# The order of the pointwise stage: two z splits and a silu earlier, the low halves of the output weight behind them

## The chip, the cores and the metric

The kernel runs on one core of a Trainium2 chip, as one program. The metric is the device time of one execution in microseconds (us); less is better. Before the change the median of three runs is 470.81 us (470.47 to 470.90).

## The reference

The reference is one layer of a hybrid streaming encoder in float32, for 1024 prompt tokens and 64 tokens of a running stream. One input projection yields queries, keys, values, two SiLU gates and a GLU pair. Group A is sliding-window attention; group B is a convolution module. Each group's output is RMS-normalised, multiplied by its gate, and both go through the shared output projection. Cut to the part around the change:

```python
def _conv_branch(u, left, conv_w, ln_g, ln_b, w_pw):
    h = _dwconv(jnp.concatenate([left, u], axis=1), conv_w)
    h = jax.nn.silu(_layernorm(h, ln_g, ln_b))
    return h @ w_pw                                   # the pointwise stage

def _merge(att, ga, conv, gb, g_att, g_conv, w_out, g_post):
    y = jnp.concatenate([_rms(att, g_att) * jax.nn.silu(ga),
                         _rms(conv, g_conv) * jax.nn.silu(gb)], axis=-1) @ w_out
    return _rms(y, g_post)
```

## The kernel before

Matrix products keep float32 accuracy by splitting each operand into a high part, rounded to the format that TensorE reads at full rate, and a low part, which is the rest (original minus high). A product is then three products: high by high, low by high and high by low. The high part of something is one copy; the low part is one subtraction with two inputs in SBUF.

The kernel has four stretches: the input projection (with the convolution's taps on VectorE beside it), attention, the pointwise stage, and the output projection, tokens in tiles of 128 (`y` in the profile, T = 0, 1, 8, 2, ..., 7).

The pointwise stage (lines 1097 to 1114) works on H, which holds the normalised convolution output, channels on the partitions, tokens along the row. Its tokens are cut into four ranges n = 0 to 3 of 280, 280, 280 and 278 columns (`LNC`), and for each range there are four output channel blocks m = 0 to 3: 16 products `pointwise(n, m)` (lines 572 to 590), written pw(n,m) below, each of 12 matmuls, which are four for high weight by zh, four for low weight by zh, four for high weight by zl. Where a range is ready, three things have been done to it:

- `S` (`silu`, line 557): four ScalarE activations on H, in place.
- `z` (`split_z`, line 562): VectorE makes zh (a copy) and zl (a subtraction). The tiles for zh and zl have two buffers each, so z2 needs the buffers of z0, which are free when pw(0,3) has been computed, and z3 those of z1, free behind pw(1,3).

Behind each product VectorE multiplies its result by the gate and puts it into H (`H<-pw,gb`), ScalarE squares the result (`csq<-pw`, for m = 0 `sqc<-pw`), and for m = 1 to 3 GpSimd adds that square to a running sum (`sqc<-sqc,csq`). The results rotate through seven PSUM banks.

Into this stage is also put the preparation of the output weight w_out, in eight pieces i = 0 to 7 (lines 1025 to 1051): `h` (`wo_hi`) is its high part on ScalarE, `l` (`wo_lo`) its low part on VectorE. Pieces 0, 3 and 6 are handled in two halves. At its end `wo_lo(i)` issues the load of piece i+3 on SyncE's DMA queue. Further tasks are `G` (gate of the attention output), `M` and `n` (high and low part, `mh` and `ml`, of the merged activations of an output tile; `M0` on ScalarE, `n0` on VectorE) and `r` (the reciprocal root of the group norm).

The order is written out by hand: the list `plan` (line 1110) has 16 entries, and entry 4n+m names the tasks that are issued directly behind pw(n,m). All instructions of this stage are pinned, that is, each engine gets its own in exactly the order in which the program issues them, and each engine works its queue in order. Before the loop z0, z1, S0, S1, the gates, piece 0 and the high part of piece 1 are already issued.

The first output product, T = 0, begins with one matmul on `mh` of the convolution half and goes on with one on `ml` of that half, which n0 writes second.

Of the kernel before, what the change touches and what calls it, by code (L numbers as in the profile page):

```python
# [48 lines left out]
def layer_kernel(ctx: ExitStack, tc: tile.TileContext, x, x_fm, w_in, w_pw, w_out, vec, g_post,  # L49
# [704 lines left out]
    h1, h2 = (0, 4), (4, KT)  # L754
# [352 lines left out]
    drain()  # L1107
    run_due(lambda p: True)

    plan = "G0,l1,h2 l2,h3 l3,S2 h4 z2 l4,h5 l5,S3 h6 z3,h7 l6,M0 l7 n0 r0 . M1 n1".split()  # L1110
    for n in range(4):
        for m in range(4):
            pointwise(n, m, [pre[PW], pre[PW + 1]])
# [136 lines left out]
```

## Time and profile before

| | |
|---|---|
| time, median of 3 runs | 470.81 us (470.47 to 470.90) |
| profiled execution, its own time | 470.69 us |
| span of that execution in the trace | 468.9 us |
| PE busy (share of the span) | 456.2 us (97%) |
| DVE busy | 380.1 us (81%) |
| ACT busy | 231.3 us (49%) |
| POOL busy | 75.0 us (16%) |
| mean granted clock of TensorE | 0.997 |

PE is TensorE's matmul, PEld its weight loads, DVE VectorE, ACT ScalarE, POOL GpSimd, SP SyncE. Times in rows are microseconds from the start of the span. L86 and L104 are helper lines through which nearly every instruction is issued, so operations are told apart by their tiles: `pw` is a result of the pointwise stage, `zh` and `zl` the split input, `wo<-woraw,vec_t` on ACT a high part of w_out, `wo<-woraw,vec_t,wo` on DVE a low part (128x1024 a whole piece, 128x512 a half), `y` the output projection. In a timeline, neighbouring instructions of one kind are merged: x4 are four, from the start of the first to the end of the last. A bracket gives the idle time in front and the instruction whose end ended it.

### The profile page before, as it was taken

To read this page: it belongs to the slowest core of one execution; us is meant where nothing else is said; L and a number is where in the kernel's file an instruction comes from. 1 tells how busy PE (TensorE), PEld (TensorE's weight loads), DVE (VectorE), ACT (ScalarE), POOL (GpSimd) and SP (SyncE) were. 2 spreads that over 40 slices of the span, in tenths; PEclk is the share of its full clock that TensorE was granted. 3 is DMA by queue.
4 is the path that set the end of the run, shared out by engine and by line. 5 is a ranking of instruction groups with operands and counts; after the bars stand their busy time and mean duration, and the time that the engine had idled before them with its cause. 6 is when DMAs were issued, how large, how long until landed. Compare 5 with 4: busy or idle time off the path is not lost.

```text
span 468.9 us, 7427 instructions
## 1 busy us (share of the span) xinstructions
PE 456.2 (97%) x2809; PEld 416.7 (89%) x2809; DVE 380.1 (81%) x672; ACT 231.3 (49%) x534; POOL 75.0 (16%) x106
## 2 busy tenths in 40 slices
PE   7999999999999999999999999999999999999994
PEld 6999999999999999998988988797899787888884
DVE  3669999999999999999899987996999547554443
ACT  6585532135032223666766856774977335333322
POOL 0000100013000000010111113254024411111100
PEclk9999999999999999999999999999999999999998
DMA  8992144035023333330101010111252212222231
GB/s 271 402 344 117 36 105 126 0 86 153 13 68 93 89 91 91 89 94 5 48 7 49 6 52 4 48 55 42 97 175 90 91 67 91 67 92 90 97 124 48
DMA packets 16491, 43.54 MB, mean 93 GB/s; under 512 B 2600, under 2 KB 4888, under 8 KB 16456
## 3 DMA queue, kind: packets, MB, share of 16 engines
q1 hardware_dynamic: 14584, 37.31, 23.4%
q0 software_dynamic: 1872, 5.77, 6.6%
q8 instruction: 22, 0.36, 0.3%
q14 instruction: 13, 0.11, 0.1%
HBM read 32.00 MB, written 4.84 MB: 79 GB/s over the span
## 4 chain that ended last, share of the span: by engine, by line
PE 85%; DVE 8%; DMA 2%; ACT 2%; issue 1%; POOL 1%; SPq 0%; DVEq 0%; POOLq 0%; ACTq 0%
PE g L104 53%; PE y L104 20%; PE av L104 3%; PE s L104 3%; DVE wo L86 2%; DVE H L86 2%; PE pa L108 2%; PE pb L108 1%; DMA x<-in_x_fm_dram 1%; DMA woraw<-in_w_out_dram 1%; DVE wlo L86 1%; POOL sqc L86 1%; DVE qb L86 1%; DVE zl L86 1%; DVE sqc L86 0%
## 5 line engine op out<-in xcount | busy, mean ns | idle before, releaser
L104 PE MATMUL g<-xT,whi 128*128 128x384 f32 (+2 forms) x960 | 222.8, 332 | 1.1 <-ACT xT L86 0.9
L104 PEld LDWEIGHTS g<-xT,whi 128*128 128x128 f32 x960 | 168.3, 188 | 8.5 <-issue 5.4
L86 DVE SCALAR_TENSOR_TENSOR H<-u,vec_t,H 128x1118 f32<-128x1118 f32 x120 | 166.6, 1388 | 3.2
L104 PE MATMUL g<-xT,wlo 128*128 128x384 f32 (+2 forms) x480 | 139.1, 332 | 0.5 <-DVE wlo L86 0.5
L104 PEld LDWEIGHTS g<-xT,wlo 128*128 128x128 f32 x480 | 88.0, 188 | 2.7 <-issue 1.2
L104 PE MATMUL y<-wo,mh 128*128 128x512 f32 (+2 forms) x304 | 89.2, 381 | 0.0
L104 PEld LDWEIGHTS y<-wo,mh 128*128 128x128 f32 (+1 forms) x304 | 55.2, 185 | 11.5
L104 PE MATMUL y<-wo,ml 128*128 128x512 f32 (+1 forms) x136 | 51.3, 379 | 0.1
L86 DVE SCALAR_TENSOR_TENSOR y<-y,small,y 128x512 f32<-128x512 f32 (+1 forms) x19 | 13.7, 721 | 31.2 <-PE y L104 29.6
L86 ACT ACTIVATE T<-T,st 128x210 f32<-128x210 f32 (+2 forms) x84 | 36.6, 450 | 4.2 <-DVE st L86 4.1
L86 POOL DMA_DIRECT2D wlo<-wraw x13 | 11.5, 885 | 148.8 <-ACT wlo L86 112.9
L104 PEld LDWEIGHTS y<-wo,ml 128*128 128x128 f32 x136 | 25.6, 188 | 4.8 <-DVE ml L86 0.4
L86 ACT ACTIVATE yj<-y 128x512 f32<-128x512 f32 (+2 forms) x21 | 12.8, 609 | 31.8 <-DVE y L86 31.7
L86 ACT ACTIVATE whi<-wraw 128x1024 fp32r<-128x1024 f32 (+1 forms) x23 | 22.4, 978 | 6.3 <-PE g L104 6.1
L104 PE MATMUL g<-xT,wq 128*128 128x384 f32 (+1 forms) x144 | 25.4, 333 | 0.0
L104 PEld LDWEIGHTS g<-xT,wq 128*128 128x128 f32 x144 | 24.2, 188 | 0.5
L86 ACT ACTIVATE sg<-g 128x384 f32<-128x384 f32 (+1 forms) x10 | 4.7, 473 | 37.1 <-PE g L104 37.1
L86 ACT ACTIVATE qb<-g 128x384 f32<-128x384 f32 (+1 forms) x12 | 5.7, 474 | 32.1 <-PE g L104 32.1
L86 DVE CUSTOM_DVE_ANT_0 T<-s,bias 128x210 f32<-128x210 f32 (+2 forms) x68 | 20.6, 359 | 0.8 <-PE s L104 0.8
L86 ACT ACTIVATE y<-y,small 128x512 f32<-128x512 f32 (+1 forms) x19 | 12.6, 666 | 16.7 <-PE y L104 16.6
L86 POOL TENSOR_TENSOR asq<-asq 128x128 f32<-128x128 f32 (+2 forms) x18 | 12.7, 707 | 38.5 <-ACT asq L86 37.8
L86 ACT ACTIVATE qb<-av 128x256 f32<-128x256 f32 x17 | 6.4, 379 | 23.6 <-PE av L104 23.6
(199 smaller groups left out, 611.3 us busy)
## 6 DMA issues: line engine op xcount, KB each, us to landing
wraw<-in_w_in_dram SPq DMA_DIRECT2D x18, 512.0 KB, 3.4
wlo<-wraw POOLq DMA_DIRECT2D x9, 512.0 KB, 4.6
H<-in_x_dram SPq DMA_DIRECT2D x8, 512.0 KB, 8.2
xr<-in_x_dram SPq DMA_DIRECT2D x8, 512.0 KB, 4.0
out_dram<-o SPq DMA_DIRECT2D x7, 512.0 KB, 2.9
woraw<-in_w_out_dram SPq DMA_DIRECT2D x5, 512.0 KB, 3.3
wraw<-in_w_in_dram SPq DMA_DIRECT2D x8, 256.0 KB, 5.6
x<-in_x_fm_dram SPq DMA_DIRECT2D x4, 384.0 KB, 5.9
```

Of the source, the lines that this page charges most:

```text
L86: ins = op(*a, **k)
L104: return tc.keep_in_program_order(nc.tensor.matmul(out, lhsT=lhsT, rhs=rhs, **k))
L108: return tc.keep_in_program_order(nc.tensor.transpose(*a, **k))
```

## The change

One line is replaced: the plan's list. Nothing else in the code differs, and the same tasks are issued.

```diff
-    plan = "G0,l1,h2 l2,h3 l3,S2 h4 z2 l4,h5 l5,S3 h6 z3,h7 l6,M0 l7 n0 r0 . M1 n1".split()
+    plan = "G0,l1,S2 h2 l2,h3 z2 l3,h4 S3,l4 h5 z3,l5 h6 h7,l6 M0,l7 n0 r0 . M1 n1".split()
```

Written out by product:

| behind | before | after |
|---|---|---|
| pw(0,0) | G0, l1, h2 | G0, l1, S2 |
| pw(0,1) | l2, h3 | h2 |
| pw(0,2) | l3, S2 | l2, h3 |
| pw(0,3) | h4 | z2 |
| pw(1,0) | z2 | l3, h4 |
| pw(1,1) | l4, h5 | S3, l4 |
| pw(1,2) | l5, S3 | h5 |
| pw(1,3) | h6 | z3, l5 |
| pw(2,0) | z3, h7 | h6 |
| pw(2,1) | l6, M0 | h7, l6 |
| pw(2,2) | l7 | M0, l7 |
| pw(2,3) to pw(3,3) | n0, r0, -, M1, n1 | the same |

## Rows read from the trace of the kernel before

**Rows 1.** Waits in 330 to 366 us: who waited for whom, total us, times, longest.
```profile
ACT csq L86 <- DVE H L86: 4.0, 4, 1.5
PEld pw L104 <- DVE zl L86: 1.5, 2, 0.8
PEld y L104 <- DVE ml L86: 0.4, 1, 0.4
```

**Rows 2.** Busy time by stretch: PE, PEld, DVE, ACT, POOL, granted clock, DMA share, GB/s.
```profile
357.10:364.40 7.30, 6.79 (x54) 6.57 (x53) 7.30 (x9) 4.17 (x8) 3.34 (x4) 1.00 0.22 72
366.00:460.00 94.00, 94.00 (x439) 77.32 (x438) 47.88 (x89) 34.73 (x74) 14.49 (x20) 1.00 0.25 87
```

**Rows 3.** Timeline of TensorE in the pointwise stage: start, length, instruction, idle in front.
```profile
348.64 0.68 PE L104 MATMUL pw<-zh,w1vT 128*128 128x280 f32 x4
349.15 0.68 PE L104 MATMUL pw<-zl,w1kT 128*128 128x280 f32 x4
350.01 0.79 PE L104 MATMUL pw<-zh,whi 128*128 128x280 f32 x4 [0.19 <-DVE zh L86]
...
351.84 0.78 PE L104 MATMUL pw<-zl,whi 128*128 128x280 f32 x4 [0.52 <-DVE zl L86]
...
358.82 0.77 PE L104 MATMUL pw<-zl,whi 128*128 128x278 f32 x4 [0.51 <-DVE zl L86]
...
365.00 0.50 PE L104 MATMUL y<-wo,ml 128*128 128x512 f32 x1
```

**Rows 4.** Timeline of VectorE in the same stage.
```profile
337.81 1.41 DVE L86 SCALAR_TENSOR_TENSOR wo<-woraw,vec_t,wo 128x512 fp32r<-128x512 f32 x2
...
344.92 1.27 DVE L86 SCALAR_TENSOR_TENSOR wo<-woraw,vec_t,wo 128x1024 fp32r<-128x1024 f32 x1
...
346.47 2.12 DVE L86 SCALAR_TENSOR_TENSOR wo<-woraw,vec_t,wo 128x512 fp32r<-128x512 f32 x2
348.52 0.79 DVE L86 TENSOR_TENSOR H<-pw,gb 128x280 f32<-128x280 f32 x2
349.23 0.73 DVE L86 CAST zh<-H 128x1120 fp32r<-128x1120 f32 x1
349.99 1.79 DVE L86 TENSOR_TENSOR zl<-H,zh 128x1120 fp32r<-128x1120 f32 x1
...
356.21 0.74 DVE L86 CAST zh<-H 128x1112 fp32r<-128x1112 f32 x1 [0.42 <-ACT H L86]
...
359.05 1.94 DVE L86 SCALAR_TENSOR_TENSOR wo<-woraw,vec_t,wo 128x512 fp32r<-128x512 f32 x2
...
363.67 1.27 DVE L86 TENSOR_TENSOR ml<-H,mh 128x512 fp32r<-128x512 f32 x1
```

**Rows 5.** Timeline of ScalarE: high part of a piece, a square, a high part in halves, a silu.
```profile
343.38 1.15 ACT L86 ACTIVATE wo<-woraw,vec_t 128x1024 fp32r<-128x1024 f32 x1
...
345.03 0.41 ACT L86 ACTIVATE csq<-pw 128x280 f32<-128x280 f32 x1 [0.51 <-DVE H L86]
345.33 1.33 ACT L86 ACTIVATE wo<-woraw,vec_t 128x512 fp32r<-128x512 f32 x2
...
346.88 2.15 ACT L86 ACTIVATE H<-H,vec_t 128x280 f32<-128x280 f32 x4
```

**Rows 6.** Timeline of GpSimd: two of the additions to the running sum.
```profile
345.52 1.33 POOL L86 TENSOR_TENSOR sqc<-sqc,csq 128x280 f32<-128x280 f32 x1 [16.39 <-ACT csq L86]
...
349.54 1.07 POOL L86 TENSOR_TENSOR sqc<-sqc,csq 128x280 f32<-128x280 f32 x1 [1.49 <-ACT csq L86]
```

**Rows 7.** Tile zl: its VectorE writes, ns min/median/max, first and last start.
```profile
L86 DVE TENSOR_TENSOR zl<-H,zh x4: 1324/1556/1794, 335.8 to 357.0; 128x1120 fp32r<-128x1120 f32 x3, 128x1112 fp32r<-128x1112 f32 x1
```

**Rows 8.** Tile woraw: its nine loads, from issue to landing.
```profile
DMA to landing us min/median/max: 2.9/3.3/4.8
```

**Rows 9.** Busy time by stretch behind the last matmul, columns as in rows 2.
```profile
462.00:465.00 3.00, 0.07 (x1) 0.00 (x0) 1.77 (x5) 0.51 (x2) 0.57 (x1) 1.00 0.00 0
466.00:468.00 2.00, 0.00 (x0) 0.00 (x0) 0.00 (x0) 0.00 (x0) 0.00 (x0) 0.50 0.68 257
```

## The prediction, made before the changed kernel was run

> **What bounds the kernel now.** I read the busy shares first, then the busy time by stretch, the waits of the pointwise stage, and last the timelines of the four engines in it.
>
> From 366 us to the end of the output projection TensorE is busy in every microsecond (94.00 of 94.00) and VectorE in half of them [rows 2]. So the end of the kernel stands at a fixed distance behind the start of the output projection: whatever moves the second matmul of T = 0 moves the time by the same amount.
>
> In the pointwise stage it is otherwise. In its last 7.3 us VectorE is busy throughout, 7.30 of 7.30, TensorE 6.79 [rows 2]. TensorE waits three times for a z part: for zh2 at 350.01, zl2 at 351.84, zl3 at 358.82 [rows 3]. Matmuls of four follow each other every 0.51 to 0.52 us (348.64, 349.15) [rows 3], so pw(2,0) could have begun at 349.67 and its zl group come at 350.71. It lost 0.34 us at zh2, some 0.7 more at zl2, and about 0.7 at zl3: 1.7 to 1.8 us together. Then the output projection waits 0.4 for `ml` [rows 1]: n0 began its second half at 363.67 and took 1.27, to 364.94, and the matmul started at 365.00 [rows 3, 4]. TensorE and VectorE therefore reach that point almost together, VectorE last. This decides the case: earlier z parts help TensorE only up to the point where n0, at the end of VectorE's queue, lets it go on.
>
> **The change part by part.** No instruction is added or removed, so the cost is in idle time and in collisions alone. I follow VectorE's queue to the end of n0, in order, with these prices: a gate product (`H<-pw,gb`) 0.36 (two in 0.79, which ends with one's full 0.43); a whole low part 1.27, and 1.20 to the next start; one in halves 1.41 undisturbed, 1.33 to the next start [rows 4]; zh 0.74; zl 1.32 undisturbed [rows 7]. On ScalarE: a square 0.30 to the next start, a whole high part 1.15, a half 0.6 to 0.7, a silu of four 2.1 [rows 5]. A square starts only when the gate product of the same result is done: ScalarE waited for `H` in front of `csq` four times, 4.0 us [rows 1]. ScalarE and VectorE thus hand work to each other in both directions.
>
> *S2 in front of h2.* ScalarE began h2 at 343.38 [rows 5]. Now S2 stands there, to 345.5; the square of pw(0,1) follows, to 345.8; then h2, to 346.95. VectorE does the gate products of pw(0,1) and pw(0,2) and is free at 344.92 + 0.36 = 345.28, where l2 is next, which needs h2. It started at 344.92 before [rows 4]; now at 347.0. VectorE stands idle 1.7 us, and all that is queued behind l2, z2 first, stands with it. Nothing covers this.
>
> *z2 behind pw(0,3).* l2 ends its turn at 348.2, the gate product of pw(0,3) at 348.56. Now collisions: GpSimd's sum begun at 345.52 during l2 (344.92 to 346.19) ended 0.66 behind l2's end; and zl2, issued at 349.99 while a sum ran to 350.61, ended 1.17 behind that, in 1.79 in place of 1.32 [rows 4, 6, 7]. I read: a sum takes some 0.65, excludes VectorE's two-input operations in SBUF, and each waits for the other. By that, the sum of pw(0,2) waits for l2 and holds zh2 to 349.5, and the sum of pw(0,3) holds zl2 to 351.33. zh2 came at 349.96 before, zl2 at 351.78. So z2 gains only 0.45 us, although it passes a gate product (pw(1,0)) and l3.
>
> *l3, l4, l5 behind them.* At 351.26 VectorE still owes the product of pw(1,0), 0.36, and l3, 1.33: less the 0.45 gained, it is 1.25 us behind. l3 runs undisturbed in this order (2.12 before, because two sums fell on it [rows 4]), which is in that figure. The products of pw(1,1) to pw(1,3) and l4 fill VectorE to 355.28.
>
> *S3 and z3.* S3 follows the square of pw(1,1), which waits for the gate product, which waits for l3: S3 runs 353.8 to 355.95, z3 waits 0.73 for it where it waited 0.42 before [rows 4]: +0.3. zh3 comes at 356.75 (before 356.95) and zl3, again with a sum on it, at 358.57 (before 358.77).
>
> *l5, h6, l6, h7, l7.* The sum of pw(1,3) is waiting when zl3 ends and goes first, so l5 is held to 359.22: +0.57. The square of pw(2,0) waits for l5 and the gate product; h6 follows it at 361.07 and l6 waits 0.8 for its first half: +0.8. l6 now runs without the sum that made it 1.94 [rows 4]: -0.52. h7 comes two squares later and l7 waits 0.3: +0.3. n0 meets the same two sums as before.
>
> *Sum:* 1.25 + 0.3 + 0.57 + 0.8 - 0.52 + 0.3 = 2.7 for the end of n0 against its time in the trace, 364.94. The same prices, laid on the old order, put n0's end 0.3 later than the trace has it, so I take 2.4. The second matmul of T = 0 starts at 367.4, though TensorE has finished the pointwise products at 364.4 and idles some 2.7 us there.
>
> The Trainium skill's page "SBUF — State Buffer" (section "SBUF: two separate sides") says that VectorE and GpSimd take the shared port pair as an exclusive lock, held for a whole instruction by whichever starts first. The zl2 row agrees (1.17 us of work behind the sum's end). For l5 the rule and the whole low parts differ: l2 ran in 1.27 with a sum begun inside it [rows 4, 6], and by that row alone l5 would be free, the total 1.8 and the time 472.5; by the rule the sum that waited gets the lock first and l5 is held.
>
> *DMAs.* l2, l3 and l4 issue the loads of pieces 5, 6 and 7 on SyncE's queue, at 348.3, 353.0 and 354.6. The slowest of the nine loads landed after 4.8 us [rows 8]: by 353.1, 357.8 and 359.4, all before h5 (356.1), h6 (361.1) and h7 (362.6). What waits behind them on that queue, the residual rows of T = 0, is needed only at its end, over 48 x 0.214 = 10 us later (439 matmuls in 94 us [rows 2]). If a load took 3 us more than the slowest, this cover would be gone for piece 6.
>
> *Bounds.* Where one collision falls differently, a sum costs up to 0.65 or nothing. Without the l5 collision and without the two short waits for h6 and h7 the total is 2.4 - 0.57 - 1.1 = +0.7; with one more collision on each of l4 and l7 it is 2.4 + 1.3 = +3.7.
>
> The profiled execution took 470.69 us, 1.8 beside its span of 468.9; 470.69 + 2.4 = 473.1. The median of the runs, 470.81, lies 0.12 higher; I stay with the profiled base.
>
> **The rivals.**
>
> A: *faster; n0 arrives in time.* The stage's new phase would avoid the collisions: in the old order they cost VectorE 0.7 (l3) + 0.47 + 0.47 (the two later zl) + 0.5 (l6) + 0.6 (second half of n0, 512 columns like half a low part, in 1.27 where that takes 0.7), 2.7 us [rows 4, 7]. If they fell away, VectorE would be back on time, the three waits for z would go (1.7) and half of that for `ml`: 470.69 - 1.9 = 468.8. It decides at the end of n0: from 364.9 downwards the change is faster. For it: the collisions are large and depend on phase. Against: there are as many sums as before, each behind its square, and the 1.7 us in front of l2 come first. 8%.
>
> B: *the backlog is mostly made up, no measurable change.* l5 free and the high parts of pieces 6 and 7 in time, plus one collision less: 0 to +0.9, about 471.2. For it: ScalarE is far from full. Against: its squares are chained to VectorE's late gate products. 11%.
>
> C: *TensorE's clock.* Behind the last matmul the granted clock still stands at 1.00 in 462 to 465 with TensorE idle and at 0.50 in 466 to 468 [rows 9]. My pause of 2.7 us before T = 0 is shorter than that first stretch; if the clock (2.4 GHz) fell to its 1.2 GHz level nevertheless, each 12 matmuls would cost 12 x 0.214 = 2.6 us more: 475.6 with one such group, 478 with two. Against it: the stretch with the wait at 358.82 has the clock at 1.00 [rows 2, 3]. 5%.
>
> D: *the list does not set the order on the engines.* Then nothing changes, 470.7. Against: the gate products, low parts and z parts stand on VectorE in the order of the plan, and the high parts and silus on ScalarE [rows 4, 5]. 2%.
>
> **How the numbers follow.** The forecast, slower by 1 to 3.7 us around 473.1, has the remaining 74%. Measurement of this kernel can tell about 0.2%, or 0.94 us, from no change. Faster by more than that: A, 8%. Within it: B and D, 13%, with a little of the forecast's lower flank (+0.7) moved there: 14% in all. Slower: 78%. The range 471.2 to 474.2 holds the forecast down to +0.5 and up to +3.5 and the upper part of B; outside lie A, D, the lower part of B, and C, some 20%.
>
> **What would show it.** Right: VectorE idle about 1.7 us in front of l2 (347.0); zh2 started at 348.6; waits for silu S3 and for the high parts of pieces 6 and 7; n0 ending near 367.4; TensorE waiting 2 to 3 us for `ml` in front of the second matmul of T = 0; the stretch behind it unchanged in length. Wrong at its first step if l2 starts before 346; wrong as a whole if n0 ends before 365.5, or if TensorE's wait for `ml` is under 1 us.

## The result

The changed kernel takes 474.67 us (median of 5 runs, 473.59 to 475.5) against 470.86 before (5 runs): ratio 1.0074, 95% interval 1.0064 to 1.0085. It is slower by 3.8 us; 2.4 was forecast, and the time lies 0.5 us above the range. The profiled execution took 474.8 us.

From the page of the profiled execution: the span, and TensorE's and VectorE's busy time.

```profile
span 473.0 us, 7427 instructions
PE 458.9 (97%) x2809; PEld 418.6 (88%) x2809; DVE 379.7 (80%) x672; ACT 231.1 (49%) x534; POOL 75.2 (16%) x106
```

VectorE has no more work than before (379.7 for 380.1). TensorE is busy 2.7 us longer with the same 2809 matmuls. Of that, 1.6 us lie behind the second matmul of T = 0 (98.66 for 97.07), where matmuls ran slower, as shown below; 0.9 lie ahead of the pointwise stage, which the change does not touch, and 0.2 in the stage.

The waits of the stage, 330 to 370 us (total, times, longest):

```profile
DVE wo L86 <- ACT wo L86: 2.4, 3, 1.5
PEld y L104 <- DVE ml L86: 2.1, 1, 2.1
...
PEld pw L104 <- DVE zl L86: 1.4, 2, 0.8
```

The first is new: VectorE waits for high parts of w_out, three times. TensorE's wait for `ml` has grown from 0.4 to 2.1 us, while the waits for zl are as long as ever (1.4 for 1.5) [rows 1].

VectorE's timeline, where [rows 4] stood before; this execution reaches the stage 0.35 us later (first pointwise matmul at 337.59 for 337.24).

```profile
344.92 0.80 DVE L86 TENSOR_TENSOR H<-pw,gb 128x280 f32<-128x280 f32 x2
347.25 1.28 DVE L86 SCALAR_TENSOR_TENSOR wo<-woraw,vec_t,wo 128x1024 fp32r<-128x1024 f32 x1 [1.54 <-ACT wo L86]
...
348.82 0.98 DVE L86 CAST zh<-H 128x1120 fp32r<-128x1120 f32 x1
349.83 1.79 DVE L86 TENSOR_TENSOR zl<-H,zh 128x1120 fp32r<-128x1120 f32 x1
...
356.17 0.74 DVE L86 CAST zh<-H 128x1112 fp32r<-128x1112 f32 x1 [0.60 <-ACT H L86]
356.94 1.78 DVE L86 TENSOR_TENSOR zl<-H,zh 128x1112 fp32r<-128x1112 f32 x1
358.65 1.80 DVE L86 SCALAR_TENSOR_TENSOR wo<-woraw,vec_t,wo 128x1024 fp32r<-128x1024 f32 x1
...
361.89 1.42 DVE L86 SCALAR_TENSOR_TENSOR wo<-woraw,vec_t,wo 128x512 fp32r<-128x512 f32 x2 [0.72 <-ACT wo L86]
...
363.83 1.28 DVE L86 SCALAR_TENSOR_TENSOR wo<-woraw,vec_t,wo 128x1024 fp32r<-128x1024 f32 x1 [0.16 <-ACT wo L86]
...
366.22 1.26 DVE L86 TENSOR_TENSOR ml<-H,mh 128x512 fp32r<-128x512 f32 x1
```

One by one the forecast's steps stand here: VectorE idle in front of l2 until h2 is done (1.54), zh2 held by a sum (0.98), z3 waiting for S3 (0.60), l5 held by a sum (1.80), l6 and l7 waiting for h6 and h7, and n0 ending at 367.48. The sum that held l5 was issued while zl3 ran and went first when zl3 ended at 358.72. It ended at 359.36, 0.64 behind zl3, and l5 another 1.09 behind it:

```profile
357.89 1.47 POOL L86 TENSOR_TENSOR sqc<-sqc,csq 128x280 f32<-128x280 f32 x1 [0.34 <-ACT csq L86]
```

TensorE's timeline, where [rows 3] stood before:

```profile
350.02 0.68 PE L104 MATMUL pw<-zh,whi 128*128 128x280 f32 x4
...
351.67 0.78 PE L104 MATMUL pw<-zl,whi 128*128 128x280 f32 x4 [0.46 <-DVE zl L86]
...
358.78 0.78 PE L104 MATMUL pw<-zl,whi 128*128 128x278 f32 x4 [0.53 <-DVE zl L86]
...
365.25 0.50 PE L104 MATMUL y<-wo,mh 128*128 128x512 f32 x1 [0.50 <-ACT mh L86]
367.54 0.51 PE L104 MATMUL y<-wo,ml 128*128 128x512 f32 x1 [1.78 <-DVE ml L86]
367.88 0.59 PE L104 MATMUL y<-wo,mh 128*128 128x512 f32 x1
368.27 0.63 PE L104 MATMUL y<-wo,ml 128*128 128x512 f32 x1
368.70 1.05 PE L104 MATMUL y<-wo,mh 128*128 128x512 f32 x2
```

The wait at zh2 is gone, the others are not. Then come the two things that cost: the second matmul of T = 0 starts at 367.54, and behind it matmuls start 0.43 us apart (368.27, 368.70) and take 0.63. The granted clock says why, in the busy time by stretch (columns as in [rows 2]; the clock stands behind POOL's busy time):

```profile
364.60:367.50 2.90, 0.66 (x4) 0.25 (x2) 2.90 (x5) 1.00 (x3) 1.97 (x2) 1.00 0.57 181
367.50:371.30 3.80, 3.76 (x10) 2.94 (x11) 3.11 (x7) 2.20 (x5) 2.62 (x3) 0.55 0.40 141
```

In 2.9 us TensorE was busy for 0.66; the clock was still granted in full. It fell only when the work had begun again, to a mean of 0.55, which is the 1.2 GHz level for most of the stretch: 10 matmuls where [rows 2] give 18 in 3.8 us (439 in 94). From the second matmul to the end of the span it is 473.0 - 367.54 = 105.46 us, where it was 468.9 - 365.00 = 103.90.

So the 4.1 us between the two spans are 0.35 from before the stage, 2.19 in the stage (367.54 - 337.59 = 29.95 for 27.76) and 1.56 from the clock. What comes ahead of the stage is no part of the change: over the profiled executions below the stage began between 336.81 and 337.76 with the same instructions in front of it, so kernels are compared by the distance from its first matmul to the second matmul of T = 0.

### The profile page after: what moved, and what is told of

Its sections match the earlier page's. It is cut to its first block, busy times and chain, and to the rows that moved or that the text cites. A ratio compares the mean times of both kernels' runs of the same rounds, so it can differ in the third digit from the quotient of the medians.

```text
span 473.0 us, 7427 instructions
## 1 busy us (share of the span) xinstructions
PE 458.9 (97%) x2809; PEld 418.6 (88%) x2809; DVE 379.7 (80%) x672; ACT 231.1 (49%) x534; POOL 75.2 (16%) x106
## 4 chain that ended last, share of the span: by engine, by line
PE 84%; DVE 8%; ACT 3%; issue 1%; DMA 1%; POOL 1%; SPq 0%; DVEq 0%; POOLq 0%; ACTq 0%
PE g L104 53%; PE y L104 21%; PE av L104 3%; PE s L104 3%; DVE wo L86 2%; DVE H L86 1%; PE pa L108 1%; PE pb L108 1%; DMA x<-in_x_fm_dram 1%; ACT H L86 1%; DVE wlo L86 1%; ACT wo L86 1%; POOL sqc L86 1%; DVE zh L86 1%; DVE zl L86 1%
## 5 line engine op out<-in xcount | busy, mean ns | idle before, releaser
L104 PE MATMUL y<-wo,mh 128*128 128x512 f32 (+2 forms) x304 | 90.4, 385 | 0.5 <-ACT mh L86 0.5
L86 POOL TENSOR_TENSOR sqc<-sqc,csq 128x280 f32<-128x280 f32 (+1 forms) x12 | 13.3, 1111 | 29.5 <-ACT csq L86 29.4
```

The lines of the kernel that those rows point to most:

```text
L86: ins = op(*a, **k)
L104: return tc.keep_in_program_order(nc.tensor.matmul(out, lhsT=lhsT, rhs=rhs, **k))
```

## The experiments

Theory: VectorE's queue delays n0 by 2.2 us, which TensorE pays in full, and the pause that this makes costs another 1 to 2 us in those executions in which the clock falls behind it. Rivals: the slow matmuls have another cause; S2 in front of h2 is the whole loss; the moved z parts themselves are.

The columns up to the distance are read from the one profiled execution of each kernel; the median is over all its runs.

| run | first pw matmul | second matmul of T = 0 | distance | median us | ratio to before, 95% |
|---|---|---|---|---|---|
| before | 337.24 | 365.00 | 27.76 | 470.86 | |
| changed | 337.59 | 367.54 | 29.95 | 474.67 | 1.0074 (1.0064 to 1.0085) |
| e1_busy_pe | 337.41 | 367.35 | 29.94 | 473.06 | 1.0051 (1.0038 to 1.0064) |
| e2_h2_first | 337.59 | 366.57 | 28.98 | 473.80 | 1.0050 (1.0032 to 1.0069) |
| e3_n0_early | 336.81 | 364.73 | 27.92 | 471.37 | 1.0011 (1.0001 to 1.0020) |
| e4_z_only | 337.53 | 365.81 | 28.28 | 471.25 | 1.0009 (1.0000 to 1.0018) |
| e5_s2_alone | 337.17 | 367.16 | 29.99 | 472.90 | 1.0043 (1.0029 to 1.0056) |
| e6_before_n0_early | 337.49 | 364.98 | 27.49 | 470.51 | 0.9994 (0.9985 to 1.0003) |
| e7_z_and_n0_early | 337.76 | 363.27 | 25.51 | 468.78 | 0.9956 (0.9944 to 0.9969) |
| e8_changed_again | 337.51 | 367.49 | 29.98 | 474.14 | 1.0067 (1.0048 to 1.0086) |
| e9_pause_filled | 337.29 | 367.29 | 30.00 | 472.91 | 1.0037 (1.0024 to 1.0050) |

The kernel before had medians of 470.81 to 470.92 beside them.

**e1_busy_pe**, the changed kernel with work in the pause:

```diff
+                if T == 0 and j == 0 and half == 1:
+                    for _ in range(5):
+                        mm(ps[:, :P], lhsT=ident, rhs=ident, start=True, stop=True)
                 for k, m, lw, rh, st, sp in parts(T, mh, ml, half):
```

> The changed kernel with five small products of the identity with itself put in front of the first matmul of T = 0, into the same PSUM tile, where the first matmul starts it anew: TensorE works through about 2.0 of the 2.7 us in which it waits for ml. Theory (n0 late by about 2.4 us, and behind the long pause the clock falls to 0.5 in some executions): the second matmul of T = 0 still starts when n0 ends, the granted clock stays 1.00, time 473.0 to 473.5, spread of the runs under 0.6 us. Rival (the slow matmuls behind the pause come from something else, such as the loads that run then, or the scatter from elsewhere): 474.2 to 475, matmuls of T = 0 still 0.43 us apart. Second rival (the pause was shorter than it looked, the dummies delay T = 0): over 475.

473.06, four of six runs within 472.9 to 473.1, the two others 473.8 and 474.4, both at a mean granted clock of 0.997, so their excess is not the clock's and its cause stays open. The useless matmuls (the trace has two for each product) were shorter than I reckoned, ten in about 1.1 us, so half of the pause stayed; the second matmul stood where it was and the next ones 0.23 to 0.25 us apart. Added work made the kernel faster, 473.06 for 474.67. That the spread would be under 0.6 did not hold.

**e2_h2_first**, the changed order with h2 and S2 in their old order:

```diff
-    plan = "G0,l1,S2 h2 l2,h3 z2 l3,h4 ...
+    plan = "G0,l1,h2 S2 l2,h3 z2 l3,h4 ...
```

> The changed order with one pair undone: h2 directly behind pw(0,0) and S2 behind pw(0,1), all else as changed. Theory: l2 starts at 345.3 and not 347, VectorE's wait of 1.5 us goes, z2 starts near 347.6 and zl2 is in time for TensorE; but VectorE then waits for S3 and for h6, and n0 still ends 1.2 us later than in the kernel before: 472.0 with the clock up, up to 473.9 with the clock fallen, because TensorE now reaches T = 0 earlier and its pause is as long, 2.9 us. Rival (S2 in front of h2 is the whole loss): 470.8 or less.

The distance is 1.22 us above the kernel before, as the theory has it: S2 in front of h2 is 0.97 of the 2.19 us, not all. The pause is as long, and the clock falls: three runs at a mean granted clock of 0.994 took 473.7 to 473.9, the one at 0.997 took 471.77. The profiled one, TensorE and then the stretch:

```profile
366.57 0.50 PE L104 MATMUL y<-wo,ml 128*128 128x512 f32 x1 [1.80 <-DVE ml L86]
366.91 0.40 PE L104 MATMUL y<-wo,mh 128*128 128x512 f32 x1
367.15 0.40 PE L104 MATMUL y<-wo,ml 128*128 128x512 f32 x1
367.38 0.77 PE L104 MATMUL y<-wo,mh 128*128 128x512 f32 x2
367.95 0.63 PE L104 MATMUL y<-wo,ml 128*128 128x512 f32 x1
```

```profile
363.70:366.50 2.80, 0.58 (x2) 0.19 (x1) 2.80 (x5) 0.92 (x2) 1.91 (x2) 1.00 0.57 187
366.50:371.20 4.70, 4.63 (x13) 3.69 (x14) 3.45 (x9) 2.58 (x6) 2.62 (x3) 0.64 0.39 115
```

Here four or five matmuls ran at full pace before they slowed down from 0.40 to 0.63: the fall follows the pause with a delay.

**e3_n0_early**, the changed order with n0 in front of l6 and l7:

```diff
-    ... h6 h7,l6 M0,l7 n0 r0 . M1 n1
+    ... h6 M0,h7 n0,l6 l7 r0 . M1 n1
```

> The changed order with M0 and n0 moved in front of h7, l6 and l7 (they are needed for T = 0's second group of matmuls only); z2, z3, S2, S3 stay where the change put them. Theory (the loss reaches the end only through n0's place at the end of VectorE's queue): n0 ends near 362 to 364.6, TensorE's pause in front of the second matmul is under 0.3 us, the clock stays at 1.00, time 470.4 to 470.9. Rival (the moved z parts and silus cost TensorE time in the stage itself): 472.5 to 474.

The pause is gone, though S2, S3 and both z stand where the change put them:

```profile
364.39 0.50 PE L104 MATMUL y<-wo,mh 128*128 128x512 f32 x1 [0.42 <-ACT csq L86]
364.73 0.39 PE L104 MATMUL y<-wo,ml 128*128 128x512 f32 x1
364.96 0.40 PE L104 MATMUL y<-wo,mh 128*128 128x512 f32 x1
```

So nearly all of the loss reaches the end through n0's place: 2.03 of the 2.19 us of distance are gone. A small wait is new, T = 0 begins 0.42 late behind the square of a pointwise product; against the old order with the same move of n0 (e6, 27.49) the distance of 27.92 is 0.43 longer. The time missed by 0.5 us: 471.37, with runs from 470.6 to 472.6. The trace is that of the fastest of them, so it does not show what made the others slower; the scatter of 2 us does not follow their clocks (0.995 to 0.998), and I did not find its cause.

**e4_z_only**, the order before with z2 and z3 one product earlier:

```diff
-    plan = "G0,l1,h2 l2,h3 l3,S2 h4 z2 l4,h5 l5,S3 h6 z3,h7 l6,M0 ...
+    plan = "G0,l1,h2 l2,h3 l3,S2 z2,h4 . l4,h5 l5,S3 z3,h6 h7 l6,M0 ...
```

> The order before with z2 and z3 alone one product earlier (directly behind pw(0,3) and pw(1,3)); S2, S3 and all low parts keep their order. Theory (VectorE is the bound at the end of the stage, and z3 now waits longer for S3): z2 0.2 to 0.4 us earlier, z3 not earlier, n0 0.3 to 0.4 later: 471.0 to 471.3. Rival (the waits for z are what the stage pays): 470.2 to 470.5.

471.25: z2 started at 349.38 (stage 0.29 later than in [rows 4], so 0.14 earlier), z3 waited 0.77 for S3, the distance grew by 0.52. Earlier z parts alone brought nothing: VectorE only does the same work in another order.

**e5_s2_alone**, the order before with S2 in front of h2:

```diff
-    plan = "G0,l1,h2 l2,h3 l3,S2 h4 z2 ...
+    plan = "G0,l1,S2,h2 l2,h3 l3 h4 z2 ...
```

> The order before with one thing changed: S2 directly in front of h2, behind pw(0,0); all z parts and low parts where they were. Theory: l2 waits about 1.7 us for h2, all behind it on VectorE comes 1.7 to 2 us later, z2 too, so TensorE's lost time is spread over zh2, zl2, zl3 and ml, no pause is over 2 us, and the clock stays at 1.00: 472.4 to 472.9, spread as in the kernel before. Rival (the clock falls whenever TensorE loses as much in the stage): 474 or more. Second rival (the idle time of VectorE is made up by fewer collisions): under 471.5.

472.90, within what was expected, by a distance of 29.99. That is in part luck, for the clock did fall, against the theory, behind a wait of 2.0 us at zh2 and one of 0.46 at zl2 (TensorE, the stretch, and the second half of n0 on VectorE):

```profile
351.76 0.76 PE L104 MATMUL pw<-zh,whi 128*128 128x280 f32 x4 [2.00 <-DVE zh L86]
352.35 0.68 PE L104 MATMUL pw<-zh,wlo 128*128 128x280 f32 x4
353.49 1.24 PE L104 MATMUL pw<-zl,whi 128*128 128x280 f32 x4 [0.46 <-DVE zl L86]
354.53 1.14 PE L104 MATMUL pw<-zh,whi 128*128 128x280 f32 x4
355.46 1.14 PE L104 MATMUL pw<-zh,wlo 128*128 128x280 f32 x4
...
366.85 0.48 PE L104 MATMUL y<-wo,mh 128*128 128x512 f32 x1
367.16 0.39 PE L104 MATMUL y<-wo,ml 128*128 128x512 f32 x1
```

```profile
353.40:357.20 3.80, 3.71 (x17) 3.71 (x18) 3.80 (x7) 3.26 (x6) 2.59 (x2) 0.55 0.31 81
```

```profile
365.31 1.28 DVE L86 TENSOR_TENSOR ml<-H,mh 128x512 fp32r<-128x512 f32 x1
```

Three fours of matmuls then took 0.93 to 1.04 us each and a fourth 0.80, where the pace is 0.52: 1.6 us together. n0 ended at 366.59, 29.42 us behind the stage's first matmul where it was 27.70 before: 1.72 later, as the theory has it. But TensorE came to T = 0 still later, and without a wait. Its second matmul stands 0.57 behind the end of n0, where it stood 0.06 behind it before, so I estimate that some 0.5 of the 1.6 us reached the end; the rest fell into time in which TensorE would have waited for VectorE. The four runs are too few to show it: at a mean clock of 0.991 and 0.994 they took 472.69 and 472.27, at 0.997 both 473.1. A fallen clock costs in full where TensorE has no slack, as at the start of the output projection; where it would have waited for VectorE, as here, it costs less.

**e6_before_n0_early**, the order before with n0 in front of l6 and l7:

```diff
-    ... z3,h7 l6,M0 l7 n0 r0 . M1 n1
+    ... z3,M0 n0,h7 l6 l7 r0 . M1 n1
```

> The order before with M0 and n0 in front of h7, l6 and l7. Theory: the wait for ml (0.4 us) goes, the three waits for z stay: 470.2 to 470.6. Rival (l6 and l7 are then late for the second group of T = 0 and take the wait over): 470.8 to 471.5.

470.51, the interval of the ratio reaches from 0.9985 to 1.0003; the distance is 0.27 smaller. The wait for `ml` was worth that much and no more, which the time alone cannot tell from nothing.

**e7_z_and_n0_early**, made from what the runs showed:

```diff
+    plan = "G0,l1,h2 S2 l2,S3 z2,h3 . l3 h4 z3 l4,h5 l5,M0 n0,h6 l6,h7 l7,r0 . M1 n1".split()
```

> A new order from what the runs showed: h2 in front of S2, S2 and S3 as early as ScalarE can, z2 directly behind pw(0,3), z3 directly behind pw(1,3), l3 to l7 behind them, and M0 and n0 in front of l6 and l7. Theory: zl2 and zl3 are in time, n0 ends near 361.3 before TensorE asks for it, the second matmul of T = 0 starts near 362.7 and not 365.0, clock at 1.00: 468.3 to 468.9. Rival (the low parts of pieces 5 to 7 are now late for T = 0's second group, and the wait moves there): 469.5 to 470.8.

468.78 (468.58 to 468.89), ratio 0.9956, faster than both kernels and than before by 2.06 us. In 340 to 460 us TensorE does not pause, and `ml` is there before it is asked for:

```profile
340.00:460.00 120.00, 120.00 (x639) 103.16 (x637) 72.94 (x127) 53.58 (x109) 25.51 (x30) 1.00 0.30 97
```

```profile
360.38 1.27 DVE L86 TENSOR_TENSOR ml<-H,mh 128x512 fp32r<-128x512 f32 x1
```

```profile
362.95 0.48 PE L104 MATMUL y<-wo,mh 128*128 128x512 f32 x1
363.27 0.39 PE L104 MATMUL y<-wo,ml 128*128 128x512 f32 x1
```

The z parts directly behind the products that free their places are here too, and TensorE waits for none of them, although z2 still waits 0.61 for S2. The whole order is worth 2.25 us of distance, where earlier z parts alone cost 0.52 (e4) and an earlier n0 alone gave 0.27 (e6): the moves pay together. What each gives in this order was not taken apart.

**e8_changed_again** is the changed kernel unaltered, on the same chip as e9.

> The changed kernel as it is, once more, to have it on one chip with the next kernel. Theory: runs whose mean granted clock is 0.996 or more take 473.0 to 474.1, runs at 0.995 or less 474.4 to 475.6, most of them the latter. Rival (clock and time are not tied): no such split.

Runs at a mean clock of 0.997: 473.01 and 473.03. At 0.993 to 0.994: 473.65, 474.62, 474.70 and 476.02. The means lie 1.73 us apart (474.75 and 473.02); the first changed runs split in the same way (0.997: 473.59, 474.03; 0.993 to 0.994: 474.67, 474.8, 475.5). Of the runs with the clock down, 473.65 fell below the bounds I had set and 476.02 above them.

**e9_pause_filled** is e1 with eleven products (`range(11)`).

> The changed kernel with eleven products of the identity with itself in front of the first matmul of T = 0 (ten of their matmul rows took 1.12 us in the run with five), so that TensorE has about 2.5 us of work in its pause of 2.7. Theory: n0 and the second matmul stand where they were, the clock stays at 1.00 in all runs, 472.9 to 473.4, which is below the changed kernel by 0.8 to 2 us though work is added. Rival (five products already did all there is to gain, and more delays the second matmul): 473.5 to 474.5.

All five runs within 472.58 to 473.0, two of them below the 472.9 expected, clocks 0.995 to 0.998. None is above the fastest of the changed kernel's runs (473.01 in e8, on the same chip). TensorE and the two stretches:

```profile
364.35 2.70 PE L104 MATMUL y<-ident 128*128 128x128 f32 x22
366.81 0.48 PE L104 MATMUL y<-wo,mh 128*128 128x512 f32 x1
367.29 0.50 PE L104 MATMUL y<-wo,ml 128*128 128x512 f32 x1
367.63 0.40 PE L104 MATMUL y<-wo,mh 128*128 128x512 f32 x1
```

```profile
364.40:367.30 2.90, 2.90 (x25) 2.58 (x25) 2.90 (x5) 0.94 (x3) 1.93 (x2) 1.00 0.60 177
367.50:371.30 3.80, 3.80 (x17) 3.09 (x17) 3.11 (x8) 3.18 (x7) 3.10 (x4) 1.00 0.43 144
```

The second matmul starts 30.00 us behind the stage's first, as in the changed kernel; behind it run 17 matmuls in 3.8 us and not 10, and from it to the end of the span it is 471.2 - 367.29 = 103.91 us, what it was before the change. 22 matmuls that compute nothing save 1.2 us at the median. With this the clock is shown to be the cause of the slow matmuls, and the loads that run at the same time are not (DMA share 0.43, as with the slow ones).

## Why the prediction was wrong

**What bounds the stage: right.** TensorE and VectorE reach the output projection almost together in the kernel before, VectorE last, and n0's place carried nearly all of the loss (e3, e6).

**The sum: right in sign, parts and size.** 2.4 was forecast, 2.19 measured. Taking off the 0.35 by which the stage began later: l2 at 346.90 (347.0 forecast), zl2 ended 351.27 (351.33), zl3 358.37 (358.57), n0 367.13 (367.4). The idle times were 1.54, 0.60, 0.72 and 0.16 us for 1.7, 0.73, 0.8 and 0.3 forecast. TensorE's matmuls waited 1.78 us for `ml` (the weight loads 2.1) and not 2 to 3, because 0.50 of the pause went to a wait that the forecast does not have, for `mh` from ScalarE (365.25); it cost nothing, since `ml` came later. The runs with the clock up, 473.0 to 474.0, lie in the range.

**The collision on l5: the rule held.** The sum that waited when zl3 ended went first, and l5 took 1.80 us for a whole low part's 1.27. The Trainium skill's "SBUF — State Buffer" (section "SBUF: two separate sides") has an exclusive lock, held for a whole instruction by whichever starts first. The trace agrees: l5 did 1.09 us of its work behind the sum's end. That a sum which waits goes ahead of VectorE's next operation does not follow from this rule alone, as the forecast took it to; the trace of l5 shows it. The row of l2 does not speak against it: l2 ran in 1.27 because there the sum came second. The collision was worth 0.53 us.

**The step that failed: that the end of the kernel stands at a fixed distance behind the start of the output projection.** By that step whatever moves the second matmul of T = 0 moves the time by the same amount, and the sum has no term for the clock. From the second matmul to the end of the span it was 105.46 us in place of 103.90, because the clock fell. The forecast had this only as rival C: the right mechanism in the right place, with 5%. I argued that the pause is shorter than the stretch behind the last matmul in which the clock stays up [rows 9], and so left C outside the range. That reads the wrong thing off those rows: they show when the clock falls if nothing comes after. In the changed kernel, e2 and e5 it fell after work had begun again (in e5 some 1.7 us after, from 351.76 to 353.49, with the wait of 0.46 between), behind unbroken waits of 1.8 to 2.0 us. In the eleven changed runs (the five of the result, and e8) the mean granted clock shows it down in seven; the price was 1.56 us in the profiled execution and 1.73 by e8's two groups, not the 2.6 of a whole group of 12 at half the clock, because only eight matmuls ran slow (those from 367.88 to 370.83, 0.43 apart where the pace is 0.23: 8 x 0.2 = 1.6). Forecast plus this price, 473.1 + 1.7 = 474.8, is the profiled execution's 474.8, but this close a match is luck: in that execution the stage cost 0.2 less than forecast and the fallen clock 0.2 less than this price, and the 0.35 from ahead of the stage makes up for both.

**The other rivals.** A (collisions vanish) did not come: zl2, zl3 and l5 each met a sum (1.79, 1.78, 1.80). B would have needed the high parts of pieces 6 and 7 in time; they were late by 0.72 and 0.16. D is excluded by the new order on every engine.

## What to carry to other kernels

Where two engines reach a join together, moving work forward in the slower one's queue bought nothing here (e4); look at what stands last in that queue in front of the join, and put the pieces that are asked for later behind it. Such a move does not show in VectorE's share of busy time (81% before and in e7), and it was worth 2 us together with what the change wanted.

A pause of TensorE like these of 2 to 3 us, ahead of a stretch that it bounds, costs more than its length in some executions; remove it, or fill it with matmuls that compute nothing. A range for a change that makes such a pause has to hold the case with the clock down.

## What was not expected of the hardware

- The granted clock stays at 1.00 through the pause and falls afterwards, in the middle of work: with the first matmuls behind it in the changed kernel, about 1 us later in e2 (between 367.38 and 367.95), 1.7 us later in e5, there behind a second, short wait. With the same code it falls in one run and not in the next (seven of eleven).
- A GpSimd sum that is already waiting gets its turn ahead of the VectorE operation that is next in VectorE's queue: l5, 1.27 us otherwise, took 1.80. The forecast counted on this, with the row of l2 against it; e2 and e3 show the same 1.80.
- Runs of one kernel at the same mean clock scatter by up to 1.8 us (e3, at 0.998) and 1.4 us (e1, at 0.997). No run shows why.
